# Band attention: turned edge blocks as float32, 128 columns wide, and one reciprocal per pair of query blocks

## The chip, the cores and the metric

The kernel runs on one core of a Trainium2 chip. The metric is the device time of one execution in microseconds (us). The engines are TensorE (PE, with its weight loads shown apart as PEld), VectorE (DVE), ScalarE (ACT), GpSimd (POOL) and SyncE (SP, which issues most transfers).

## What is computed

A trunk of two layers over 1024 tokens of width 1024. In each layer, a modulated RMSNorm, one input projection, three groups of attention heads (64 wide) side by side, an RMSNorm per group, one output projection with a gated residual, and a gated feed-forward part. The attention is what the change touches:

```python
# group A: 4 heads, 2-D neighbourhood (8 x 16) with a relative bias
# group B: 6 heads on 2 key heads, |i - j| <= 128, a sink logit, a shared relative bias
# group C: 6 heads on 2 key heads, dense
s = jnp.einsum('bnqgrd,bnkgd->bngrqk', qb, kb).astype(jnp.float32) * scale + bias
s = jnp.where(valid[None, :, None, None], s, NEG_INF)
p = jax.nn.softmax(jnp.concatenate([s, sink_logits], axis=-1), axis=-1)[..., :-1]
o = jnp.einsum('bngrqk,bnkgd->bnqgrd', p.astype(v.dtype), vb)
```

Groups A and B are the band groups: a block of 128 queries sees only its own block of 128 keys and the two next to it.

## The kernel before

**Precision.** Most products are made in float32r, a float32 format that the array multiplies at reduced precision. An operand that needs more is split into a rounded part and the rest (`split_pt`: ACT copies and rounds, DVE subtracts), and both parts are multiplied. Where an operand is declared plain float32, the array multiplies it as it is.

**The attention stage.** It walks through 64 pairs of query blocks per layer: 24 of group C (6 heads, 4 pairs each), then 16 of A and 24 of B. A pair p of a head is the query blocks 2p and 2p + 1, 256 columns in all. Each pair passes four steps: `qk` (scores on PE, the mask and bias or the row maximum on DVE, the exponential with its row sum on ACT, once for each of the two blocks c = 0, 1), the division (`divide`: a reciprocal on DVE, then `scale_rows` on POOL), `turn` (PE transposes the 128 x 128 blocks into PSUM, the copies bring them back) and `pv` (PE multiplies them by the values into the tile pv; `products` holds the loop, `combine` adds the two halves of the heads).

**The loop.** Iteration n turns pair n, multiplies pair n - 1 and scores pair n + 3 (group C) or n + 5 (band groups). Each iteration has two halves, i = 0, 1. What `finish` has put on the list `unfinished` is issued in the next half iteration, so the division of block c = 0 comes in the second half of an iteration and that of block c = 1 in the first half of the next. Only POOL's order is fixed as written in this stage (`pin((pool,), True)`); the instructions of the other engines are placed by a scheduler, and each engine then runs its own list in order.

**A band pair.** Of the four blocks of keys that a pair sees, the two inner ones are seen by both query blocks, the left outer one only by the first and the right outer one only by the second: these are the edges. Pairs p = 1, 2 have both edges, p = 0 only the right one, p = 3 only the left one. `turn(0)` turns the four inner blocks into one PSUM tile T and splits them into pt (two parts of 256 columns for each key block). `turn(1)` turns the one or two edges and splits them into the tile `edge`. Its two buffers are made once by `edges_make` (at n = 8) with the half that the edge does not fill set to zero, so that an edge is multiplied 256 columns wide like the inner blocks, rounded part and rest:

```python
movs = [(k0 + i, self.pt[0][:, i, :], self.pt[1][:, i, :]) for i in range(2)]
if self.left:
    movs.append((k0 - 1, e[:, 0, 0, :], e[:, 1, 0, :]))
if self.right:
    movs.append((k0 + 2, e[:, 0, 1, :], e[:, 1, 1, :]))
```

All engine calls pass through one helper, so that nearly all instructions of the profile carry line 49; the tiles tell them apart (sC, sA, sB: scores; pr: exponentials; rs: maxima, sums and reciprocals; T, pt, edge: turned blocks; pv, cmb, y: results).

Of the kernel before, what the change touches and what calls it, by code (L numbers as in the profile page):

```python
# [10 lines left out]
F32 = mybir.dt.float32  # L11
F32R = mybir.dt.float32r
# [7 lines left out]
P = 128  # L20
# [56 lines left out]
def f32(ap):  # L77
    return ap.bitcast(F32)
# [7 lines left out]
def trunk(ctx: ExitStack, tc, A, C, out):  # L86
    nc = tc.nc
    pe, act, dve, pool, sp = (
        Engine(tc, e) for e in (nc.tensor, nc.scalar, nc.vector, nc.gpsimd, nc.sync)
    )  # L90
# [28 lines left out]
    ident = idp.tile([P, P], F32, name="ident")  # L119
# [6 lines left out]
    ident, ones = f32(identr), f32(onesr[:, 0:1])  # L126
# [692 lines left out]
    for l in range(2):  # L819
# [212 lines left out]
        vs = vsp.tile([P, 8, 8, P], F32R, name="vs")  # L1032
# [95 lines left out]
        def scale_rows(pr, r):  # L1128
            pool.tensor_scalar(
                out=pr, in0=pr, scalar1=r, scalar2=1.0, op0=ALU.mult, op1=ALU.mult  # L1130
            )
# [14 lines left out]
                pr, s, AF.Exp, bias=rs[:, c : c + 1], accum_out=rs[:, 2 + c : 3 + c]  # L1146
            )

        def divide(pr, rs, c):
            dve.reciprocal(rs[:, 4 + c : 5 + c], rs[:, 2 + c : 3 + c])  # L1150
            scale_rows(pr, rs[:, 4 + c : 5 + c])

        first_pairs = []

        def early_scores():

            p = len(first_pairs)
# [11 lines left out]
            return lambda: [divide(prs[c], rs, c) for c in range(2)]  # L1169

        for oc in range(NE, 8):
            w = wab
            for half in range(2):
# [15 lines left out]
                i = 2 * (oc - NE) + half  # L1189
# [31 lines left out]
        zB = [bz_tile() for _ in range(2)]  # L1221
        pad(atp, 16)
        gss = {23: gss_tile()}
        edge = []

        def edges_make():
            for _ in range(2):
                e = atp.tile([P, 2, 2, 256], F32R, name="edge", tag="edge", bufs=2)
                for z in range(2):
                    pool.memset(f32(e[:, z, 0, 128:256]), 0.0)  # L1230
                    pool.memset(f32(e[:, z, 1, 0:128]), 0.0)
                edge.append(e)

        edges_used = [0]

        def next_edge():
            edges_used[0] += 1
            return edge[edges_used[0] % 2]

        def edge_ap(e, z, left, right):  # L1240
            flat = e[:, z, :, :].rearrange("p e q -> p (e q)")
            if left and right:
                return flat.rearrange("p (a q) -> p a q", a=4)[:, 0:4:3, :]
            return flat[:, None, 0:128] if left else flat[:, None, 384:512]

        def pt_tile():
            return wp.tile([P, 4, 256], F32R, name="pt", tag="whl", bufs=8)

# [3 lines left out]
        def rs_tile():  # L1252
            return atp.tile([P, 8], F32, name="rs", tag="rs", bufs=6)
# [4 lines left out]
        def split_pt(T, hi, lo):  # L1258
            act.copy(hi, T)
            dve.tensor_tensor(out=lo, in0=T, in1=f32(hi), op=ALU.subtract)  # L1260

        class Pair:
# [5 lines left out]
            def __init__(self, row, vh, p):  # L1268
                self.row, self.vh, self.p = row, vh, p
                self.rs = rs_tile()  # L1270

            def finish(self, c, pr):

                unfinished.append(lambda: divide(pr, self.rs, c))

            def products(self, movs, part):
                if part == 0:
                    if self.p % 2 == 0:
                        open_pv[0] = psV.tile([P, H], F32, name="pv", tag="V")
                    self.pvt = open_pv[0]  # L1280
                cols = slice((self.p % 2) * 256, (self.p % 2) * 256 + 256)
# [47 lines left out]
        class PairC(Pair):  # L1329
# [5 lines left out]
            def qk(self, c):  # L1335
                pr = self.pr[c] = pr_tile()
                c_scores(self.h, 2 * self.p + c, c, pr, self.rs)
                self.finish(c, pr)

            def turn(self, c):  # L1340
                if c == 0:
# [9 lines left out]
            def pv(self, part):  # L1351
                self.products(
                    [
                        (kb * 4 + i, self.pt[kb][0][:, i, :], self.pt[kb][1][:, i, :])
                        for kb in range(2)
                        for i in range(4)
                    ],
                    part,
                )
# [38 lines left out]
        class Band(Pair):  # L1398
# [10 lines left out]
            def qk(self, c):  # L1409
                rs, p, sk = self.rs, self.p, self.sk  # L1410
                if c == 0:
                    self.s = psS.tile([P, 2, 512], F32, name=self.name, tag="S")
                s, pr = self.s, self.pr
                j = 2 * p + c
                a, b = self.spans[c]
                for i in range(2):
                    pe.matmul(
                        s[:, c, a:b], self.q[:, j * P : (j + 1) * P],
                        self.k[i][:, (j - 1) * P + a : (j - 1) * P + b],
                        start=(i == 0), stop=(i == 1),  # L1420
                    )
# [12 lines left out]
                self.finish(c, pr[:, c, a:b])  # L1434

            def turn(self, c):
                pr = self.pr
                T = t_tile()
                if c == 0:
                    self.pt = [pt_tile() for _ in range(2)]  # L1440
                    for b in range(2):
                        for i in range(2):
                            pe.transpose(
                                T[:, 2 * b + i, :], pr[:, b, (1 - b + i) * P : (2 - b + i) * P],
                                ident,
                            )
# [6 lines left out]
                ne = 0  # L1453
                if self.left:
                    pe.transpose(T[:, ne, :], pr[:, 0, 0:P], ident)
                    ne += 1
                if self.right:
                    pe.transpose(T[:, ne, :], pr[:, 1, 2 * P : 3 * P], ident)
                    ne += 1
                split_pt(  # L1460
                    T[:, 0:ne, :],
                    edge_ap(e, 0, self.left, self.right),
                    edge_ap(e, 1, self.left, self.right),
                )

            def pv(self, part):
                k0, e = 2 * self.p, self.e
                movs = [(k0 + i, self.pt[0][:, i, :], self.pt[1][:, i, :]) for i in range(2)]
# [128 lines left out]
        for n in range(-AHEAD - 1, N + 1):  # L1597
# [22 lines left out]
                    (v_back if n else v_store)(j)  # L1620
            if n == 50:
                yq = qk_tile()
            if n == 8:
                edges_make()
            if n == 54:
                wst = [w_o_stage(k) for k in korder[:2]]
            if n in (55, 59):
# [735 lines left out]
```

## Time and profile before

| | us |
|---|---|
| median of 3 runs | 2432.55 (2431.05 to 2435.31) |
| the profiled execution | 2435.83 |
| its span, first to last instruction | 2434.1 |
| band groups of layer 0 in it, about | 375 to 487 |
| group C and band groups of layer 1, about | 1440 to 1570 and 1570 to 1685 |

The profile shows one execution. A group row reads: engine, operation, out<-in, sizes, xcount | busy us, mean ns of one | idle time of the engine just before them and what ended it. A wait row reads: who waited <- for whom: us in total, times, the longest. A chain row gives the share of the chain of work that ended last, by engine and tile. In rows of time, the start and the length of a run of like instructions stand first.

### The profile page before, as it was taken

The numbers are of one execution on the slowest core, as the hardware profiler recorded it, in microseconds if no ns is written. First come the engines' busy times: TensorE is split into PE (matmuls) and PEld (weight loads), VectorE is DVE, ScalarE is ACT, GpSimd is POOL, SyncE is SP. The second block draws the span as 40 slices with busy tenths as digits, with TensorE's granted clock in tenths as the row PEclk, the third lists the DMA queues.
The fourth block names the chain that finished last, engine by engine and source line by source line (L and its number), as shares of the span: only waits on it lengthen the run. The fifth ranks groups of instructions, "written<-read, shape, count | busy, mean of one in ns | idle before, by whom it ended". The sixth has DMA issues, their size and how long they took to land.

```text
span 2434.1 us, 33735 instructions
## 1 busy us (share of the span) xinstructions
PE 2362.9 (97%) x11733; PEld 1963.3 (81%) x11733; DVE 1785.1 (73%) x2950; ACT 1203.9 (49%) x2290; POOL 759.6 (31%) x741
## 2 busy tenths in 40 slices
PE   8999999999999999999999999999999999999998
PEld 5778888788788788788787879987877888888886
DVE  5756899976967788586677589998787545547865
ACT  3421788954543333344543148887454333334443
POOL 1530344620244444300036114464004444430001
PEclk9999999999999999999999999999999999999999
DMA  8478215154245454596434861242534422329643
GB/s 262 151 237 269 61 27 148 43 181 148 87 143 178 156 183 150 166 276 195 144 96 113 277 187 27 58 125 68 191 96 136 142 100 96 103 101 305 206 129 108
DMA packets 305338, 356.98 MB, mean 147 GB/s; under 512 B 51964, under 2 KB 221788, under 8 KB 305168
## 3 DMA queue, kind: packets, MB, share of 16 engines
q1 hardware_dynamic: 283296, 342.07, 44.5%
q10 hardware_dynamic: 21504, 12.59, 2.0%
q8 instruction: 93, 1.52, 0.3%
q14 instruction: 77, 0.63, 0.1%
q0 software_dynamic: 368, 0.17, 0.0%
HBM read 269.79 MB, written 88.63 MB: 147 GB/s over the span
## 4 chain that ended last, share of the span: by engine, by line
PE 50%; DVE 4%; issue 4%; ACT 2%; POOL 1%; DMA 1%; ACTq 0%; SPq 0%; POOLq 0%; DVEq 0%
PE ps_w L49 21%; PE ps_d L49 14%; PE ps_o L49 3%; PE pv L49 2%; PE ps_ab L49 2%; PE ps_v L49 2%; PE T L49 2%; PE sC L49 2%; DMA qkd<-qko 1%; ACT pr L49 1%; PE ps_c L49 1%; POOL ct L49 1%; DVE pt L49 0%; PE ps_st L49 0%; DVE pr L49 0%
## 5 line engine op out<-in xcount | busy, mean ns | idle before, releaser
L49 PE MATMUL ps_d<-wpt 128*128 128x512 f32 x1848 | 424.3, 390 | 2.2 <-ACT wpt L49 1.9
L49 PEld LDWEIGHTS ps_d<-wpt 128*128 128x128 f32 x1848 | 345.6, 188 | 76.2 <-issue 3.0
L49 POOL TENSOR_SCALAR pr<-pr,rs 128x1024 f32<-128x1024 f32 (+2 forms) x248 | 192.8, 780 | 228.8 <-DVE rs L49 203.2
L49 POOL TENSOR_TENSOR sg<-sg,u 128x512 f32<-128x512 f32 x86 | 125.8, 1465 | 356.5 <-ACT sg L49 117.9
L49 PE MATMUL pv<-pt,vs 128*128 128x256 f32 x1088 | 182.5, 296 | 10.8 <-DVE y L49 3.6
L49 ACT CAST wpt<-w 128x512 fp32r<-128x512 f32 x154 | 95.7, 621 | 179.9 <-PE ps_d L49 161.4
L49 DVE TENSOR_TENSOR pt<-T,pt 128x512 fp32r<-128x512 f32 x272 | 178.2, 681 | 6.9 <-ACT pt L49 5.1
L49 PE MATMUL T<-identr,pr 128*128 128x128 f32 x1176 | 172.8, 273 | 1.0 <-DVE pt L49 0.5
L49 ACT CAST pt<-T 128x512 fp32r<-128x512 f32 x272 | 153.0, 586 | 37.8 <-PE T L49 35.8
L49 ACT COPY u<-ps_w 128x512 f32<-128x512 f32 x128 | 75.1, 587 | 193.1 <-PE ps_w L49 192.9
L49 POOL TENSOR_TENSOR wpt<-ws,wpt 128x512 fp32r<-128x512 f32 x80 | 112.3, 1405 | 179.0 <-ACT wpt L49 132.5
L49 DVE TENSOR_TENSOR wpt<-w,wpt 128x512 fp32r<-128x512 f32 x154 | 108.9, 707 | 80.6 <-ACT wpt L49 78.4
L49 PEld LDWEIGHTS pv<-pt,vs 128*128 128x128 f32 x1088 | 145.3, 189 | 27.6 <-DVE y L49 9.8
L49 PEld LDWEIGHTS T<-identr,pr 128*128 128x128 f32 x1176 | 138.2, 140 | 18.3 <-POOL pr L49 1.3
L49 DVE SCALAR_TENSOR_TENSOR acc<-wmt,condT,acc 128x512 f32<-128x512 f32 (+1 forms) x98 | 116.9, 1201 | 44.2 <-DMA wmt<-in_w_mod_dram 43.7
L49 ACT CAST wpt<-ws 128x512 fp32r<-128x512 f32 x176 | 107.7, 622 | 63.4 <-issue 28.2
L49 DVE TENSOR_TENSOR wpt<-ws,wpt 128x512 fp32r<-128x512 f32 x96 | 82.3, 868 | 62.9 <-ACT wpt L49 62.8
L49 DVE TENSOR_TENSOR wpt<-graw,wpt 128x512 fp32r<-128x512 f32 x154 | 109.2, 709 | 19.3 <-ACT wpt L49 19.3
L49 ACT CAST wpt<-graw 128x512 fp32r<-128x512 f32 x154 | 95.0, 617 | 48.2 <-DMA graw<-gpd 40.3
L49 DVE TENSOR_TENSOR ws<-wr 128x512 f32<-128x512 f32 x88 | 80.0, 911 | 49.2 <-POOL wpt L49 46.0
L49 PE MATMUL ps_w<-h22h,wpt 128*128 128x512 f32 x352 | 111.6, 399 | 4.3 <-ACT sg L49 3.6
L49 DVE TENSOR_REDUCE rs<-sC 128x1 f32<-128x1024 f32 x88 | 107.1, 1218 | 7.1 <-PE sC L49 5.2
(299 smaller groups left out, 6024.5 us busy)
## 6 DMA issues: line engine op xcount, KB each, us to landing
wr<-in_w_gu_dram SPq DMA_DIRECT2D x92, 512.0 KB, 4.1
gpd<-sg SPq DMA_DIRECT2D x154, 256.0 KB, 4.4
graw<-gpd SPq DMA_DIRECT2D x76, 512.0 KB, 3.5
w<-in_w_down_dram SPq DMA_DIRECT2D x110, 256.0 KB, 5.4
wmt<-in_w_mod_dram SPq DMA_DIRECT2D x48, 512.0 KB, 6.1
qk<-qkd SPq DMA_DIRECT2D x44, 512.0 KB, 6.7
wst<-in_w_o_dram SPq DMA_DIRECT2D x32, 512.0 KB, 3.9
wmt<-in_w_mod_dram SPq DMA_DIRECT2D x64, 256.0 KB, 3.8
```

Source lines behind the costliest of these rows:

```text
L49: ins = op(*args, **kwargs)
```

## The change

The tile `edge` becomes plain float32, 128 columns for each edge, allocated for each pair from three buffers; the zero halves and `edges_make` go. A turned edge is copied once out of PSUM, by ACT for odd p and by DVE for even p, with no split. `products` takes for each key block the columns of the result and a list of moving operands: two parts of 256 columns for an inner block, one float32 operand of 128 columns for an edge, multiplied with the values read as plain float32. `divide` takes both blocks of a pair: `finish` gathers them and, after the second one, puts one division on the list, with one reciprocal over two columns and then the two scalings on POOL. This holds for all three groups.

```diff
-        def divide(pr, rs, c):
-            dve.reciprocal(rs[:, 4 + c : 5 + c], rs[:, 2 + c : 3 + c])
-            scale_rows(pr, rs[:, 4 + c : 5 + c])
+        def divide(prs, rs):
+            dve.reciprocal(rs[:, 4:6], rs[:, 2:4])
+            for c, pr in enumerate(prs):
+                scale_rows(pr, rs[:, 4 + c : 5 + c])
...
-            def finish(self, c, pr):
-
-                unfinished.append(lambda: divide(pr, self.rs, c))
+            def finish(self, pr):
+
+                self.parts.append(pr)
+                if len(self.parts) == 2:
+                    unfinished.append(lambda: divide(self.parts, self.rs))
...
-                for n, (kc, a, b) in enumerate(movs):
+                for n, (kc, at, mvs) in enumerate(movs):
                     if (n < half) != (part == 0):
                         continue
-                    for i, mv in enumerate((a, b)):
+                    for i, mv in enumerate(mvs):
+                        v = vs[:, kc, self.vh, :]
                         pe.matmul(
-                            self.pvt[:, cols], vs[:, kc, self.vh, :], mv,
-                            start=(n == 0 and i == 0), stop=(n == len(movs) - 1 and i == 1),
+                            self.pvt[:, c0 + at.start : c0 + at.stop],
+                            v if mv.dtype == F32R else f32(v), mv,
...
-                e = self.e = next_edge()
...
-                split_pt(
-                    T[:, 0:ne, :],
-                    edge_ap(e, 0, self.left, self.right),
-                    edge_ap(e, 1, self.left, self.right),
-                )
+                e = self.e = atp.tile([P, 2, P], F32, name="edge", tag="edge", bufs=3)
...
+                if self.p % 2:
+                    act.copy(e[:, 0:n], T[:, 0:n])
+                else:
+                    dve.tensor_copy(e[:, 0:n], T[:, 0:n])
...
-                    movs.append((k0 - 1, e[:, 0, 0, :], e[:, 1, 0, :]))
+                    movs.append((k0 - 1, slice(0, P), [e[:, 0]]))
...
-                    movs.append((k0 + 2, e[:, 0, 1, :], e[:, 1, 1, :]))
+                    movs.append((k0 + 2, slice(P, 2 * P), [e[:, int(self.left)]]))
```

More of the change, by code (lines that the diff above doesn't have):

```diff
@@ L1168, in early_scores @@
             first_pairs.append(prs)
-            return lambda: [divide(prs[c], rs, c) for c in range(2)]
+            return lambda: divide(prs, rs)
         for oc in range(NE, 8):
@@ L1223, in trunk @@
         gss = {23: gss_tile()}
[L1224 to L1244, printed above, removed]
         def pt_tile():
@@ L1270, in __init__ @@
                 self.rs = rs_tile()
-            def finish(self, c, pr):
-                unfinished.append(lambda: divide(pr, self.rs, c))
+                self.parts = []
+            def finish(self, pr):
+                self.parts.append(pr)
+                if len(self.parts) == 2:
+                    unfinished.append(lambda: divide(self.parts, self.rs))
             def products(self, movs, part):
@@ L1280, in products @@
                     self.pvt = open_pv[0]
-                cols = slice((self.p % 2) * 256, (self.p % 2) * 256 + 256)
+                c0 = (self.p % 2) * 256
                 half = (len(movs) + 1) // 2
-                for n, (kc, a, b) in enumerate(movs):
+                for n, (kc, at, mvs) in enumerate(movs):
                     if (n < half) != (part == 0):
                         continue
-                    for i, mv in enumerate((a, b)):
+                    for i, mv in enumerate(mvs):
+                        v = vs[:, kc, self.vh, :]
                         pe.matmul(
-                            self.pvt[:, cols], vs[:, kc, self.vh, :], mv,
-                            start=(n == 0 and i == 0), stop=(n == len(movs) - 1 and i == 1),
+                            self.pvt[:, c0 + at.start : c0 + at.stop],
+                            v if mv.dtype == F32R else f32(v), mv,
+                            start=(n == 0 and i == 0),
+                            stop=(n == len(movs) - 1 and i == len(mvs) - 1),
+                            skip_group_check=True,
                         )
@@ L1337, in qk @@
                 c_scores(self.h, 2 * self.p + c, c, pr, self.rs)
-                self.finish(c, pr)
+                self.finish(pr)
             def turn(self, c):
@@ L1353, in pv @@
                     [
-                        (kb * 4 + i, self.pt[kb][0][:, i, :], self.pt[kb][1][:, i, :])
+                        (kb * 4 + i, slice(0, 256), [t[:, i, :] for t in self.pt[kb]])
                         for kb in range(2)
@@ L1433, in qk @@
                 )
-                self.finish(c, pr[:, c, a:b])
+                self.finish(pr[:, c, a:b])
             def turn(self, c):
@@ L1451, in turn @@
                     return
-                e = self.e = next_edge()
[L1453 to L1459, printed above, removed]
-                split_pt(
-                    T[:, 0:ne, :],
-                    edge_ap(e, 0, self.left, self.right),
-                    edge_ap(e, 1, self.left, self.right),
-                )
+                e = self.e = atp.tile([P, 2, P], F32, name="edge", tag="edge", bufs=3)
+                n = 0
+                for left, here in ((True, self.left), (False, self.right)):
+                    if here:
+                        src = pr[:, 0, 0:P] if left else pr[:, 1, 2 * P : 3 * P]
+                        pe.transpose(T[:, n, :], src, ident)
+                        n += 1
+                if self.p % 2:
+                    act.copy(e[:, 0:n], T[:, 0:n])
+                else:
+                    dve.tensor_copy(e[:, 0:n], T[:, 0:n])
             def pv(self, part):
                 k0, e = 2 * self.p, self.e
-                movs = [(k0 + i, self.pt[0][:, i, :], self.pt[1][:, i, :]) for i in range(2)]
+                movs = [
+                    (k0 + i, slice(0, 2 * P), [t[:, i, :] for t in self.pt]) for i in range(2)
+                ]
                 if self.left:
-                    movs.append((k0 - 1, e[:, 0, 0, :], e[:, 1, 0, :]))
+                    movs.append((k0 - 1, slice(0, P), [e[:, 0]]))
                 if self.right:
-                    movs.append((k0 + 2, e[:, 0, 1, :], e[:, 1, 1, :]))
+                    movs.append((k0 + 2, slice(P, 2 * P), [e[:, int(self.left)]]))
                 self.products(movs, part)
@@ L1622, in trunk @@
                 yq = qk_tile()
-            if n == 8:
-                edges_make()
             if n == 54:
```

## The prediction

> **What bounds the kernel now.** I read the page first (busy shares, then the chain that ended last), then the stretches of time by engine, then the chain inside the stretches that the change touches.
>
> ```profile
> span 2434.1 us, 33735 instructions
> ...
> PE 2362.9 (97%) x11733; PEld 1963.3 (81%) x11733; DVE 1785.1 (73%) x2950; ACT 1203.9 (49%) x2290; POOL 759.6 (31%) x741
> ...
> PE 50%; DVE 4%; issue 4%; ACT 2%; POOL 1%; DMA 1%; ACTq 0%; SPq 0%; POOLq 0%; DVEq 0%
> ```
>
> Over the whole span TensorE leads. But these are averages over stages, and the change lives in the attention stage of each layer. The next view is the busy time by engine in three stretches: the band groups of layer 0, those of layer 1, and the dense group (C) of layer 1. Columns: stretch, its length, then PE, PEld, DVE, ACT, POOL.
>
> ```profile
> 375.00:487.00 112.00, 105.75 (x746) 92.75 (x745) 102.06 (x361) 101.36 (x277) 65.89 (x118) 1.00 0.38 103
> 1570.00:1682.00 112.00, 105.05 (x732) 91.23 (x731) 102.23 (x358) 101.51 (x277) 68.53 (x118) 1.00 0.34 94
> 1450.00:1570.00 120.00, 119.23 (x857) 108.30 (x856) 113.38 (x192) 102.95 (x191) 53.27 (x55) 1.00 0.14 36
> ```
>
> In the band groups VectorE is busy 91% and ScalarE 91% of the time, and PE has holes although its busy time counts pipelined matmuls long. In group C PE has no holes at all (119.2 of 120). The chain by line says who ends last: first the band groups of layer 1 (1570 to 1682), then their last third (1643 to 1665), then group C (1450 to 1570).
>
> ```profile
> by line: PE pv L49 14.7%; ACT pr L49 12.9%; PE T L49 7.5%; DVE pr L49 7.1%; issue 7.0%; PE sB L49 5.9%; PE sA L49 5.1%; DVE pt L49 4.8%; ACT pt L49 4.1%; POOL y L49 3.4%; POOL pr L49 3.3%; DVE y L49 3.0%; PE ps_st L49 3.0%; ACT cmb L49 2.9%
> ...
> by line: ACT pr L49 32.4%; ACT pt L49 12.7%; issue 12.1%; ACT cmb L49 9.4%; ACT edge L49 6.3%; POOL y L49 5.7%; ACT qk L49 5.7%; POOL pr L49 3.3%; ACT rb L49 2.8%; DVE pt L49 2.7%; PE pv L49 2.7%; ACT gss L49 2.5%; DVE pr L49 1.8%; DVE rs L
> ...
> by line: PE pv L49 33.9%; PE sC L49 29.6%; PE T L49 26.9%; DVE rs L49 2.2%; ACT pr L49 1.5%; DVE y L49 1.1%; issue 1.1%; DVE pt L49 1.0%; ACT pt L49 1.0%; ACT cmb L49 1.0%; PE sA L49 0.9%; DVEq L49 0.0%
> ```
>
> Group C is PE's. The band groups are nobody's: the chain changes hands, with stretches that are nearly all ScalarE. The first row names 84.7% of its chain: ACT 19.9 (pr, pt, cmb), DVE 14.9, PE 36.2. Scaled to the whole (divided by 0.847) and to 112 us, that is about 26.3 us on ACT, 19.7 us on DVE and 47.9 us on PE in one layer's band groups.
>
> **The edge copies.** There are 40 band pairs in a layer, 20 with one edge block and 20 with two. Now ACT rounds each turned edge out of PSUM and DVE subtracts to get the rest; after the change one of the two engines makes one plain copy, ACT for odd pairs (p = 1 with two blocks, p = 3 with one), DVE for even ones.
>
> ```profile
> L49 ACT CAST edge<-T 128x256 fp32r<-128x256 f32 x40 | 14.8, 369 | 1.9 <-PE T L49 1.4
> L49 ACT CAST edge<-T 128x128 fp32r<-128x128 f32 x40 | 10.5, 263 | 5.4 <-PE T L49 5.4
> L49 DVE TENSOR_TENSOR edge<-T,edge 128x256 fp32r<-128x256 f32 x40 | 16.5, 411 | 0.0
> L49 DVE TENSOR_TENSOR edge<-T,edge 128x128 fp32r<-128x128 f32 x40 | 11.2, 281 | 0.1
> ...
> L49 DVE COPY xt<-ps_x 128x512 f32<-128x512 f32 x4 | 2.5, 682 | 0.0
> L49 DVE TENSOR_TENSOR pt<-T,pt 128x512 fp32r<-128x512 f32 x272 | 178.2, 681 | 6.9 <-ACT pt L49 5.1
> ```
>
> ACT per layer: 20 x (0.369 + 0.263) = 12.6 us go, 10 x (0.369 + 0.263) = 6.3 us come (a plain copy in place of a rounding one, taken at the same price): 6.3 us less, 6.2% of its 101.5. DVE per layer: 20 x (0.411 + 0.281) = 13.8 us go. A DVE copy out of PSUM takes as long as the subtraction of the same size (682 and 681 ns at 512 columns), so 10 x (0.411 + 0.281) = 6.9 us come: 6.9 us less.
>
> **The reciprocals.** 64 pairs in a layer, each with two, now each with one over two columns.
>
> ```profile
> L49 DVE RECIPROCAL rs<-rs 128x1 f32<-128x1 f32 x248 | 38.8, 158 | 14.7 <-ACT pr L49 10.0
> ...
> L49 DVE RECIPROCAL gm<-gm 128x8 f32<-128x8 f32 x1 | 0.2, 203 | 0.4 <-ACT gm L49 0.4
> ```
>
> Two columns lie between one (158) and eight (203); by their slope it is 164 ns, so a pair saves 0.152 us: 6.1 us for the 40 band pairs and 3.6 us for the 24 of group C, all on DVE. With the edges DVE loses 13.0 us, 12.7% of its 102.2, in each layer's band groups.
>
> The merged reciprocal adds a wait: it stands in DVE's queue behind the exponential of the second block, and the mask additions, maxima and subtractions queued after it wait with it. The division factor of the first block comes later by one exponential and its read, 0.618 + 0.193 us, and POOL, whose order is fixed, then scales both blocks in one go, ahead of the sink columns of later pairs.
>
> ```profile
> L49 ACT ACTIVATE pr<-pr,rs 128x385 f32<-128x385 f32 x72 | 44.3, 618 | 0.7 <-POOL pr L49 0.6
> L49 ACT ACTIVATION_READ_ACCUMULATOR pr<-pr,rs 128x1 f32 x160 | 30.8, 193 | 0.0
> ...
> DVE rs L49 <- ACT pr L49: 4.3, 13, 0.5
> PEld T L49 <- POOL pr L49: 0.6, 3, 0.3
> ```
>
> The last two rows are waits in 1570 to 1682 (total, times, longest). A band pair is scored five pairs before it is turned, and a pair takes 112 / 40 = 2.8 us, so 14 us stand against 0.8 us of lateness: I book nothing. The DVE wait may halve with the number of reciprocals or double with their lateness: between -2 and +4 us a layer, taken as 0, because the merged instruction is issued half an iteration later than the first one was.
>
> **The edge products on PE.** 120 edge blocks in both layers. Now two float32r multiplications of 256 columns each (rounded part and rest, with a zero half); afterwards one float32 multiplication of 128 columns. What does float32 cost? The trace has three kinds of it: turns (T, one record for each call), row sums (ps_st, 48 calls in the code and 96 records) and the modulation rows (ps_mod from gm, 8 calls and 16 records). So a float32 product is two records, each with a weight load. Rows below are weight loads or matmuls in order of time: start, length of the run, count.
>
> ```profile
> L49 PE MATMUL ps_st<-onesr,gss 128*128 128x1 f32 x96 | 11.0, 245 | 0.0
> L49 PE MATMUL ps_mod<-gm,condT 128*1 128x512 f32 x16 | 8.2, 591 | 0.0
> ...
> 14.55 1.02 PE L49 MATMUL ps_mod<-gm,condT 128*1 128x512 f32 x2
> ...
> 403.35 1.93 PEld L49 LDWEIGHTS ps_st<-onesr,gss 128*128 128x128 f32 x16
> ...
> 343.34 0.68 PEld L49 LDWEIGHTS T<-identr,pr 128*128 128x128 f32 x6
> 343.99 1.01 PEld L49 LDWEIGHTS pv<-pt,vs 128*128 128x128 f32 x8
> ...
> 432.78 0.55 PEld L49 LDWEIGHTS pv<-edge,vs 128*128 128x128 f32 x4
> ```
>
> Streaming: 1.02 - 0.591 = 0.43 us for 512 columns of a float32 record, so 0.107 for 128. Loading: float32 loads follow each other every (1.93 - 0.19) / 15 = 0.116 us; turns, which stream 128 float32 columns behind each load, every (0.68 - 0.14) / 5 = 0.108; the float32r products every (1.01 - 0.19) / 7 = 0.117, the edge ones 0.12. Loads and streams overlap in all of them. A new edge record should take the longer of 0.116 and 0.107, as the old one does, and there are 240 of either: 0. The lower bound is the turns' pace, 240 x -0.009 = -2 us; the upper, if this kind does not overlap, 240 x 0.107 = +26 us. I take 0: ps_st has the same loads and T the same streams.
>
> The Trainium skill, page "TensorE: Matmul & The Clock Gate", section "The mechanism", says that a weight load overlaps running matmuls only where the row groups differ; these use all rows, so by it the record would cost load plus stream, and the sum the upper bound. The rows of T and pv speak against it here. The page "FP8 and Floating Point Precision" of the Trainium skill, section "TensorE Precision Notes", gives a true float32 product four passes; with a load of its own for each, 4 x 0.116 us stand against 2 x 0.117. The ps_st rows show two loads for a product, not four.
>
> **Small things.** 16 memsets go from POOL, which is busy 61% of the band groups and off the path; nothing is booked. Three edge buffers stand where there were two, and a turned edge's PSUM tile is free after one reader instead of two in a row. Waits for the edges were small (ACT for the turn, PE for the edges):
>
> ```profile
> ACT edge L49 <- PE T L49: 3.1, 9, 0.6
> PEld pv L49 <- ACT edge L49: 0.8, 1, 0.8
> PEld pv L49 <- DVE edge L49: 0.8, 2, 0.6
> ```
>
> That is 1.6 us of PE in a layer, inside the sum below.
>
> **The sum.** In the band groups the time that the chain spends on ACT and DVE shrinks with their load: 26.3 x 6.2% = 1.6 us, 19.7 x 12.7% = 2.5 us, together 4.1 us a layer. In group C DVE holds 4.3% of the chain (rs, y, pt), 5.2 us of 120, and loses 3.6 / 113.4 = 3.2%: 0.2 us. Two layers: 8.6 us, call it 8.8 with the halved edge waits. Nothing outside the attention stage changes. The profiled execution took 2435.83 us (span 2434.1 and 1.7 around it), 3.3 above the median 2432.55 of the three timed runs; I expect 2427.0 of a profiled execution and 2423.8 of the median. A difference of 0.2% (4.9 us) is about what a measurement of this kernel can tell from none.
>
> **Rivals.**
> *ACT sets the pace throughout.* The stretch 1643 to 1665 is that: three quarters of the chain are ACT and its issue gaps. If the whole of the band groups went with ACT's load, 2 x 6.3 = 12.6 us would go: 2420; with all of group C's DVE saving as well (7.2 us), 2413. Against it: PE holds 43% of the chain.
> *No change.* The instructions of group C and of the band groups are placed by a scheduler, and their order on every engine differs from the second C pair on (the built programs show it). The holes that ACT and DVE leave may be filled by waits for PE: 2428 to 2437, centre 2432.
> *Slower through PE.* Float32 loads and streams of the edges do not overlap: +12.9 us of PE a layer. PE's 732 records at 0.12 are 88 us of 112 and would become 101. By PE's share of the chain that costs 5.5 us, at most 12.9, less the 4.3 gained: +2 to +17 over both layers, taken as +10: 2442.6. It decides from 4.3 / 0.43 / 120 = 0.083 us more a record, a pace of 0.20. The turns and row sums speak against it.
> *Slower through the late division.* POOL's fixed order makes each pair's turn wait. At half of the longest such wait seen, 0.15 us for 128 pairs, 19 us come and 8.8 go: 2443. It decides from 0.07 us a pair. Against it: the lead of five pairs, in group C three.
>
> **How the numbers follow.** The forecast 0.44, ACT throughout 0.20, no change 0.20, PE 0.09, late division 0.07. Faster by over 0.2%: 0.64; within: 0.20; slower: 0.16. The range runs from most of the second case, 2414, over the forecast and the no-change case to 2436, and leaves out the two slower cases and the far ends.
>
> **What would show it.** In the changed profile: edge copies 20 + 20 on each of ACT and DVE at about 369 / 263 and 411 / 281 ns; 128 reciprocals near 164 ns; edge records of PE 240, their loads 0.116 to 0.12 us apart (0.2 or more means the PE rival); ACT's busy time in the band groups about 95 us, DVE's about 89, in a stage about 4 us shorter; group C unchanged within 1 us. PE turns waiting for POOL by more than some 5 us a layer would mean the late division. The forecast is wrong if ACT and DVE fall as said and the stage keeps its length.

## The result and the profile after

The changed kernel takes 2423.16 us (median of 10 runs, 2420.56 to 2430.54), the kernel before 2432.93 us (10 runs, 2429.54 to 2438.49) beside it: a ratio of 0.9965, 95% interval 0.9954 to 0.9975, or 9.8 us less. The forecast was 2423.8. The profiled execution took 2422.97 us. Its page, the lines that answer to those of before:

```profile
span 2421.1 us, 33439 instructions
...
PE 2350.5 (97%) x11733; PEld 1955.2 (81%) x11733; DVE 1766.8 (73%) x2782; ACT 1194.3 (49%) x2250; POOL 753.4 (31%) x725
...
PE 48%; DVE 4%; issue 4%; DMA 2%; ACT 2%; POOL 2%; ACTq 0%; SPq 0%; POOLq 0%; DVEq 0%
```

Over the span little shows. What can be measured well is the length of a stage between two marks. For the band groups I take the first score of group A (tile sA) and the start of the last copy of a head's half (tile cmb). The rows by tile give lowest / median / highest duration in ns, then the first and the last start. Layer 0, before and then after:

```profile
L49 PE MATMUL sA<-qk x64: 278/339/446, 374.7 to 420.5; 128*128 128x384 f32 x48, 128*128 128x256 f32 x16
L49 ACT COPY cmb<-pv x32: 577/581/587, 271.9 to 505.2; 64x512 f32<-64x512 f32 x32
```

```profile
L49 PE MATMUL sA<-qk x64: 278/338/446, 375.2 to 419.1; 128*128 128x384 f32 x48, 128*128 128x256 f32 x16
L49 ACT COPY cmb<-pv x32: 577/582/584, 272.8 to 498.6; 64x512 f32<-64x512 f32 x32
```

That is 505.2 - 374.7 = 130.5 us before and 498.6 - 375.2 = 123.4 after; in layer 1, by the same marks, 130.3 and 123.2. So the band groups are 7.1 us shorter in each layer, where 4.1 was forecast. Busy time in these very stretches (stretch, length, then PE, PEld, DVE, ACT, POOL), before and after:

```profile
374.70:505.20 130.50, 122.37 (x848) 106.57 (x847) 119.37 (x388) 113.69 (x301) 72.77 (x123) 1.00 0.36 102
```

```profile
375.20:498.60 123.40, 117.81 (x843) 103.86 (x842) 111.61 (x328) 108.91 (x281) 71.65 (x124) 1.00 0.38 108
```

DVE issues 60 instructions fewer (20 for the edges, 40 reciprocals), ACT 20 fewer. The shares hardly move (DVE 91 to 90%, ACT 87 to 88%, PE 94 to 95%): the same mixture runs faster, and no engine has taken over. The durations of the instructions that changed, grouped by shape, in the band groups of layer 0 after:

```profile
L49 PE MATMUL pv<-edge,vs 128*128 128x128 f32 x120 | 20.2, 274 | 0.0
L49 PEld LDWEIGHTS pv<-edge,vs 128*128 128x128 f32 x120 | 17.0, 190 | 0.0
L49 DVE RECIPROCAL rs<-rs 128x2 f32<-128x2 f32 x41 | 6.5, 160 | 1.4 <-ACT pr L49 1.1
L49 DVE COPY edge<-T 128x256 f32<-128x256 f32 x10 | 4.2, 415 | 0.0
L49 ACT COPY edge<-T 128x256 f32<-128x256 f32 x10 | 3.6, 364 | 0.4 <-PE T L49 0.4
L49 DVE COPY edge<-T 128x128 f32<-128x128 f32 x10 | 2.8, 277 | 0.0
L49 ACT COPY edge<-T 128x128 f32<-128x128 f32 x10 | 2.6, 262 | 0.6 <-PE T L49 0.6
```

These are the prices of the prediction (369/263 on ACT, 411/281 on DVE, 164 for the reciprocal). The weight loads of the edge products, in order of time, four in a row:

```profile
440.49 0.53 PEld L49 LDWEIGHTS pv<-edge,vs 128*128 128x128 f32 x4
```

That is (0.53 - 0.19) / 3 = 0.113 us from one to the next, no more than before (0.12). The chain in most of the band groups of layer 1 (1560 to 1672), and the waits there (1565 to 1670; who waited <- for whom: us, times, longest):

```profile
by line: PE pv L49 15.8%; ACT pr L49 14.2%; POOL pr L49 8.8%; issue 8.1%; PE T L49 8.0%; ACT pt L49 5.6%; PE sA L49 5.6%; ACT cmb L49 4.0%; DVE pr L49 3.9%; DVE pt L49 3.7%; DVE y L49 3.1%; PE sB L49 3.1%; PE ps_st L49 3.0%; POOL y L49 2.2%
```

```profile
POOL pr L49 <- DVE rs L49: 33.7, 21, 6.1
...
DVE rs L49 <- ACT pr L49: 1.1, 4, 0.3
...
PEld T L49 <- POOL pr L49: 0.4, 1, 0.4
```

DVE's share of the chain (pr, pt, y) falls from 14.9 to 10.7%, and POOL's scaling rises from 3.3 to 8.8%. But PE's turns wait for POOL no more than before (0.4 us, and 0.6 between 1565 and 1670 before), and DVE's wait for the exponential shrinks (1.1 us, 3.7 before).

Group C became longer, which was not forecast. I count it from the first product of a turned block (tile pv) to the first score of group A: before 257.8 to 374.7 in layer 0 and 1444.6 to 1561.5 in layer 1, 116.9 us in both; after 117.9 and 119.4.

### The profile page after: what moved, and what is told of

It is laid out like the page before. It is cut to its first block, busy times and chain, and to the rows that moved or that the text cites. A ratio compares the mean times of both kernels' runs of the same rounds, so it can differ in the third digit from the quotient of the medians.

```text
span 2421.1 us, 33439 instructions
## 1 busy us (share of the span) xinstructions
PE 2350.5 (97%) x11733; PEld 1955.2 (81%) x11733; DVE 1766.8 (73%) x2782; ACT 1194.3 (49%) x2250; POOL 753.4 (31%) x725
## 4 chain that ended last, share of the span: by engine, by line
PE 48%; DVE 4%; issue 4%; DMA 2%; ACT 2%; POOL 2%; ACTq 0%; SPq 0%; POOLq 0%; DVEq 0%
PE ps_w L49 21%; PE ps_d L49 14%; PE ps_o L49 3%; PE pv L49 2%; PE T L49 2%; PE ps_v L49 2%; PE sC L49 2%; DMA qkd<-qko 1%; ACT pr L49 1%; PE ps_c L49 1%; POOL ct L49 1%; PE ps_ab L49 0%; DVE acc L49 0%; DMA graw<-gpd 0%; POOL pr L49 0%
## 5 line engine op out<-in xcount | busy, mean ns | idle before, releaser
L49 POOL TENSOR_SCALAR pr<-pr,rs 128x1024 f32<-128x1024 f32 (+2 forms) x248 | 187.0, 768 | 227.8 <-DVE rs L49 212.8
L49 POOL TENSOR_TENSOR sg<-sg,u 128x512 f32<-128x512 f32 x86 | 125.5, 1461 | 354.5 <-ACT sg L49 117.9
L49 POOL TENSOR_TENSOR wpt<-ws,wpt 128x512 fp32r<-128x512 f32 x80 | 111.6, 1395 | 180.8 <-ACT wpt L49 133.9
L49 PEld LDWEIGHTS pv<-pt,vs 128*128 128x128 f32 x1088 | 143.9, 189 | 21.1 <-DVE y L49 11.1
L49 PEld LDWEIGHTS T<-identr,pr 128*128 128x128 f32 x1176 | 139.9, 140 | 19.7 <-ACT edge L49 2.2
```

What stands on the lines that cost most here:

```text
L49: ins = op(*args, **kwargs)
```

## The experiments

Three theories stood: that ACT and DVE share the pace with PE (the forecast), that ACT alone sets it, and that PE's edge records cost or save something. Later a fourth came, on group C. All lengths in us, layer 0 / layer 1. "By the stages" is the change of the band groups and of group C against the kernel before, both layers added up, from one profile; "timed" is the difference of the medians of runs on the same chip (the kernel before stood at 2433.67 beside e0 to e3, 2436.12 beside e4 to e7, 2433.11 beside e8 to e11).

| kernel | median | ratio to before, 95% | band groups | group C | by the stages | timed |
|---|---|---|---|---|---|---|
| before | 2432.93 | | 130.5 / 130.3 | 116.9 / 116.9 | | |
| changed | 2423.16 | 0.9965, 0.9954 to 0.9975 | 123.4 / 123.2 | 117.9 / 119.4 | -10.7 | -9.8 |
| e0 changed, again | 2422.60 | 0.9960, 0.9946 to 0.9974 | 123.7 / 123.4 | 119.5 / 117.9 | -10.1 | -11.1 |
| e1 edges only | 2430.20 | 0.9986, 0.9972 to 0.9999 | 126.9 / 126.8 | 119.9 / 117.7 | -3.3 | -3.5 |
| e2 reciprocal only | 2430.44 | 0.9981, 0.9969 to 0.9992 | 128.7 / 129.9 | 116.4 / 116.4 | -3.2 | -3.2 |
| e3 merged in bands only | 2424.79 | 0.9959, 0.9943 to 0.9974 | 123.3 / 123.6 | 118.4 / 120.0 | -9.3 | -8.9 |
| e4 edges all on ACT | 2424.45 | 0.9944, 0.9917 to 0.9971 | 124.4 / 124.4 | 117.8 / 119.4 | -8.6 | -11.7 |
| e5 edges all on DVE | 2424.30 | 0.9959, 0.9942 to 0.9975 | 126.1 / 125.8 | 117.9 / 117.9 | -6.9 | -11.8 |
| e6 float32, 256 wide | 2434.99 | 1.0002, 0.9987 to 1.0017 | 128.6 / 128.5 | 116.4 / 116.4 | -4.7 | -1.1 |
| e7 float32r, 128 wide | 2433.62 | 0.9994, 0.9984 to 1.0005 | 129.0 / 128.6 | 116.5 / 116.4 | -4.1 | -2.5 |
| e8 pool size kept | 2417.52 | 0.9943, 0.9927 to 0.9959 | 123.5 / 123.6 | 116.4 / 116.4 | -14.7 | -15.6 |
| e9 inner float32, even pairs | 2423.20 | 0.9960, 0.9945 to 0.9975 | 124.4 / 124.4 | 116.4 / 116.4 | -13.0 | -9.9 |
| e10 inner float32, all pairs | 2442.42 | 1.0033, 1.0020 to 1.0046 | 134.9 / 134.7 | 116.4 / 116.4 | +7.8 | +9.3 |
| e11 changed, third time | 2423.45 | 0.9965, 0.9951 to 0.9978 | 123.3 / 123.2 | 119.4 / 119.7 | -9.0 | -9.7 |

Stage lengths of the changed kernel agree within 0.5 us over three profiles, in the band groups, while whole runs scatter by several us. The two last columns agree within 1 us in seven rows and differ by 1.5 to 4.9 in the other six: the stretch from the last copy cmb of layer 0 to the first score of layer 1, which no edit touches, alone takes 913 to 927 us in the 14 profiles. So the stages carry the fine verdicts and the medians the coarse ones. The texts on record count group C from its first score, which takes in the end of the projections; that end (19 to 23 us) scatters by more than what is looked for, so the table leaves it out. This mark was chosen after e8, not before.

**e0: the changed kernel again**, no edit, as the reference beside e1 to e3.

> The changed kernel as it is, as the yardstick beside the others on one chip. It measured 2423.2 against 2432.9 (ratio 0.9965). Both theories expect 0.995 to 0.998 of the kernel before, the band groups from the first sA to the last combine about 123.3 us long in both layers (130.4 before) and group C of layer 0 from the first sC to the first sA about 140.4 (139.1 before).

The band groups repeat at 123.7 / 123.4. Group C is long again, but in the other layer.

**e1: the edges alone.** The division as before (its main line; `divide` too is that of before).

```diff
...
-                    unfinished.append(lambda: divide(self.parts, self.rs))
+                unfinished.append(lambda: divide(pr, self.rs, c))
```

> The float32 edges alone; every block keeps its own reciprocal and division. Theory 1 (the load taken from ACT and DVE sets the gain, edges and reciprocals alike): ACT loses 6.3 us a layer and DVE 6.9, by my shares of the chain 1.6 + 1.3 = 2.9 of 4.1 us a layer; scaled to the 7.1 that the trace shows, about 5.0 us a layer, 10 less in all for the band groups, 0 in group C (its order on PE is that of before up to the first band pairs): 2423. Theory 2 (the merged reciprocal costs in group C by its later division and brings its gain in the band groups): 7 us a layer minus what the reciprocals brought, group C back at 139.1; 2420 to 2424. Rival (the edges brought nothing and the new order of the merged division brought it all): 2432.

The band groups lose 3.5 us a layer: more than the 2.9 that the shares of the chain gave, less than the 5.0 scaled up from the whole change (and 2430.20 in all where 2423 was expected). Group C is longer although nothing in its work differs from before: whatever lengthens it is not the merged reciprocal.

**e2: the reciprocal alone.** The kernel before, with the merged `divide` and `finish`.

```diff
-            dve.reciprocal(rs[:, 4 + c : 5 + c], rs[:, 2 + c : 3 + c])
+            dve.reciprocal(rs[:, 4:6], rs[:, 2:4])
...
```

> The merged reciprocal alone, in all three groups; the edges stay in two float32r parts of 256 columns. Theory 1: DVE loses 6.1 us a layer in the band groups, worth 19.7 x 6% = 1.2, scaled by 7.1 / 4.1 about 2 us a layer; group C gains 0.2 a layer: 2428 to 2429. Theory 2: group C becomes 1.3 us longer in each layer and the band groups gain 1 to 2: 2431 to 2433, group C of layer 0 at 140.4. Rival: 2423, the whole of the gain.

1.8 and 0.4 us less in the band groups (forecast: 1.2 by the share, 2 scaled up), 0.5 less in group C (forecast: 0.2). With e1 that makes 4.6, but both together give 7.1: the merged reciprocal is worth 1.1 us beside the old edges and 3.5 beside the new ones. The two layers differ by 1.2 us in this profile, so the 1.1 is rough.

**e3: edges as changed, reciprocal merged in the band groups alone.**

```diff
...
+                self.parts.append(pr[:, c, a:b])
+                if c:
+                    unfinished.append(lambda: divide_pair(self.parts, rs))
```

> Float32 edges, the merged reciprocal in the band groups and one reciprocal for each block in group C. Theory 1 (group C's 1.3 us more is an accident of the order, worth nothing): the same as the changed kernel within 1.5 us, 2423. Theory 2 (the merged division costs in group C): group C of layer 0 back at 139.1 and the band groups at 123.3: 1.3 us a layer better than the changed kernel, about 2420.5.

The band groups have the whole gain (123.3 / 123.6), so all of it is made there; group C, with its old division, is long (118.4 / 120.0).

**e4 and e5: all edge copies on one engine.**

```diff
-                if self.p % 2:
-                    act.copy(e[:, 0:n], T[:, 0:n])
-                else:
-                    dve.tensor_copy(e[:, 0:n], T[:, 0:n])
+                act.copy(e[:, 0:n], T[:, 0:n])            # e4
+                dve.tensor_copy(e[:, 0:n], T[:, 0:n])     # e5
```

> The changed kernel with every edge copied by ACT. ACT's load is that of the kernel before (12.6 us of edge copies a layer), DVE loses 13.8 + 6.1. Theory 1 (both engines' loads count, each by its share of the chain): the band groups of the changed kernel, 123.4 us, become about 2.5 us longer by ACT and 2 us shorter by DVE: 123 to 125, all in all 2423 to 2426. Rival (ACT sets the pace): +6.3 us a layer, band groups 128 to 130, 2435. Rival (DVE sets it): 117 to 120 and 2415.

> The changed kernel with every edge copied by DVE. ACT loses 12.6 us a layer against the kernel before, DVE only 6.1. Theory 1: 123 to 125 in the band groups, 2423 to 2426. Rival (ACT sets the pace): 117 to 119, 2412. Rival (DVE sets it): 129 to 130, 2436.

Against the changed kernel the band groups are 1.1 us longer with all copies on ACT and 2.6 us longer with all on DVE. Theory 1 had 123 to 125 for both: e4 lies in it (124.4), e5 above it (126.1 / 125.8), but below the 129 of its rival. If either engine alone set the pace, clearing it wholly would have been the best of the three; the even split is. Against e2 (both engines loaded, the same reciprocals) e5 takes 12.6 us of rows off ACT for 3.3 us of stage, 0.27 a us; e4 takes 13.8 us off DVE for 4.9, 0.36 a us. These prices are no constants: by them the even split would gain 6.3 x 0.27 + 6.9 x 0.36 = 4.2 us on e2, and it gains 6.0.

**e6: float32 edges, kept 256 columns wide** with a zero half (the line for a left edge; the right one and three prepared buffers likewise).

```diff
...
-                    movs.append((k0 - 1, slice(0, P), [e[:, 0]]))
+                    movs.append((k0 - 1, slice(0, 2 * P), [e[:, 0]]))
```

> The changed kernel with float32 edges 256 columns wide (three prepared buffers with a zero half): the same copies and divisions, twice the streamed columns. A record then streams 256 float32 columns, 0.213 us by the modulation rows, in place of loading for 0.116: about 0.1 us more for 120 records a layer, 12 us of PE. Theory 1 (PE holds some 43% of the chain): the band groups become 5 us longer, 128 to 129, at most 12 (135); 2433. Rival (PE has slack and waits for the others anyway): 123 to 125, no change against the changed kernel. It also shows the pace of such records: 0.21 us.

The row of the edge products by tile, and four of their loads in a row:

```profile
L49 PE MATMUL pv<-edge,vs x240: 377/379/382, 393.7 to 1694.6; 128*128 128x256 f32 x120
...
443.51 0.74 PEld L49 LDWEIGHTS pv<-edge,vs 128*128 128x128 f32 x4
```

A record takes 379 ns, in the changed kernel 275 (median): 120 x 0.104 = 12.5 us of PE more a layer, and four loads take 0.74 us in place of 0.53. The band groups are 5.2 us longer than the changed kernel's: 0.42 us for each us of PE, where PE's share of the chain had said 0.43. This is the price of the rival "slower through PE", paid; the changed kernel doesn't pay it.

**e7: the edges as two float32r parts, 128 columns wide.**

```diff
...
+                split_pt(T[:, 0:n], e[:, 0, 0:n], e[:, 1, 0:n])
```

> The changed kernel with the edges split into two float32r parts as before (ACT rounds, DVE subtracts) but multiplied 128 columns wide, no zero half; merged reciprocal kept. The copies cost what they did before. Theory 1 (the copies are the gain and PE pays the weight load either way, 0.116 us a record): like the merged reciprocal alone, band groups 128.7 to 130, 2430. Rival (the width is the gain): 123 to 125, 2424. If a float32r record of 128 columns takes longer than 0.116 us, its pace shows it, and the band groups grow by PE's share of it.

```profile
L49 PE MATMUL pv<-edge,vs x240: 220/275/310, 392.0 to 1686.9; 128*128 128x128 f32 x120
...
448.94 0.53 PEld L49 LDWEIGHTS pv<-edge,vs 128*128 128x128 f32 x4
```

Half the width, and the record is as long as a float32 one of 128 columns (275), hardly shorter than 256 columns of float32r (282); the loads stand 0.113 us apart, as in the changed kernel. The band groups stand at 129, as in e2, which has the same copies: the width alone brings hardly anything (0.5 us on average), the gain is in the copies.

**e8: the changed kernel with the attention pool kept at its old size.** The smaller edge buffers (3 KB a partition in place of 8) move the tiles that are allocated after them by 5120 bytes. In e6 and e7 they move them by 2048. An unused tile puts the 5120 bytes back.

```diff
+            if n == 8:
+                atp.tile([P, 1280], F32, name="hold")
```

> The changed kernel with an unused tile of 1280 columns in the attention pool, so that the pool has the size of before and its tiles the addresses of before. In all kernels whose edge buffers take 3 KB (the changed one, edges alone, all on ACT, all on DVE) group C runs 279 to 282 us in the two layers together; in those with 6 or 8 KB 275 to 276. Their traces show DVE's first row maximum of layer 0's group C waiting 1.4 us for the stores of the query-key tile (qkd from qko): the tile rs lies on the last stored buffer there, on the one before in the others. Theory 1 (the addresses cause it): that wait goes, group C takes 275 to 277 in both layers, the band groups stay at 123.3: about 4 us less than the changed kernel, 2419. Rival (group C's length is scatter of the transfers): 279 to 282 again, 2423.

The trace had named a wait: the first row maximum of group C waits for a store of the projections' results (DVE in order of time; in brackets the idle time before and who ended it). After, then e8:

```profile
259.43 2.36 DVE L49 TENSOR_REDUCE rs<-sC 128x1 f32<-128x1024 f32 x2 [1.38 <-DMA qkd<-qko]
```

```profile
258.28 2.35 DVE L49 TENSOR_REDUCE rs<-sC 128x1 f32<-128x1024 f32 x2
```

By the addresses of the built programs, which no view of the profile shows, the tile rs falls on a buffer of qko, which holds results on their way out: in the kernel before on the last but one to be stored, in the changed kernel on the last one. The wait of 1.0 to 1.9 us stands in both layers of the changed kernel, e0, e1, e3, e4, e5 and e11, and in none of before, e2, e6, e7, e8, e9, e10. It delays the first exponentials, and so PE's next scores (PE's loads, after and e8):

```profile
261.95 0.76 PEld L49 LDWEIGHTS sC<-qk 128*128 128x128 f32 x4 [2.38 <-ACT pr L49]
```

```profile
260.79 0.77 PEld L49 LDWEIGHTS sC<-qk 128*128 128x128 f32 x4 [0.91 <-ACT pr L49]
```

In e8 the wait is gone and group C takes 116.4 us in both layers. The table shows the same split everywhere: 116.4 to 116.9 in the 14 layers without the wait, 117.7 to 120.0 in the 14 with it, on average 2.3 more. The timed medians say 5.9 us for both layers (e8 beside e11), the stages of the two profiles 5.7. The intervals of the ratios overlap, but five of the six runs of e8 (2415.82 to 2418.80) are below the fastest of the 24 runs of the changed kernel (2420.56). Two things in the e8 profile speak the other way. By the length from the first score, which the expectation used, it shows no gain: 139.7 and 139.8 us, the 279 to 282 of the rival. The part ahead of the first product takes 23.3 and 23.4 us there at a mean granted clock of 0.93, like layer 1 of e11 (23.3 us, 0.93); in the other 25 layers it takes 19.4 to 22.5 at 1.00. And the profiled execution of e8 is as long as that of e11 (2426.77 and 2426.50 us), because the stretch between the two attention stages took 920.7 us in it against 915.6; why isn't shown. The gain is thus well seen in group C and in the timed runs, its size less so. e8 is the fastest version of all: 15.6 us below the kernel before.

**e9 and e10: inner blocks as float32 too**, on top of e8, in even pairs or in all: one plain copy by ACT in place of the split, the products then float32, 256 wide.

```diff
+                    plain = self.p % 2 == 0     # e10: True
+                    if plain:
+                        t = self.pt[0] = f32(self.pt[0])
+                        act.copy(...)
+                        return
```

> The kernel with the kept pool size, and in even band pairs the inner blocks too are copied once as float32, by ACT, and multiplied as float32 (two records of 256 columns for each key block). Per layer 20 subtractions of 0.681 us leave DVE (13.6 us) and PE streams about 0.1 us more for 80 records (7.7 us). Theory 1 (each engine's load counts by its measured price: DVE about 0.36 us per us, PE 0.40): -4.9 + 3.1 = 1.8 us less a layer, band groups 121.5, 2415.5. Rival (with DVE and ACT relieved PE sets the pace): the band groups grow by up to 7 us, 125 to 130, 2423 to 2432.

> The same in all band pairs: 27 us less on DVE, 15.4 us more on PE a layer, DVE at some 62 of 105 us, PE's load and stream time at 103 of about 120. Theory 1 at the measured prices: -9.8 + 6.2 = 3.6 us less a layer, 120; but PE would then be busy 86% of it and its price rises: 120 to 128. Rival (PE sets the pace): 128 to 138 and 2428 to 2448.

Busy time in 105 us of the band groups of layer 0: e8, e9, e10.

```profile
375.00:480.00 105.00, 101.27 (x739) 90.50 (x740) 93.80 (x301) 95.36 (x257) 64.32 (x115) 1.00 0.41 110
```

```profile
375.00:480.00 105.00, 102.17 (x712) 91.80 (x711) 85.50 (x284) 94.45 (x255) 64.58 (x117) 1.00 0.37 100
```

```profile
375.00:480.00 105.00, 102.81 (x685) 91.33 (x683) 73.04 (x251) 88.12 (x234) 60.06 (x104) 1.00 0.40 110
```

DVE falls from 89% to 81 and 70%, and the stage does not get shorter: 0.9 us longer in e9, 11.3 in e10. e9 (124.4) lies between theory 1 (121.5) and its rival (125 to 130), e10 (134.9) in the range of the rival. e10's records of the inner blocks take 379 ns in place of 282, 160 of them in a layer: 15.5 us more on PE, so a us of PE now costs 0.73, after whatever the relief of DVE brings, and PE is busy 131.2 of the 134.9 us of the stage. The rival "PE sets the pace" is real, and begins just past the change.

**e11: the changed kernel a third time**, beside e8 to e10.

> The changed kernel beside the last three on the same chip, as their yardstick: 2422 to 2424, band groups 123.4, group C 279 to 282 in both layers together.

It repeats: 123.3 / 123.2, the wait in both layers, 2423.45.

## Why the prediction was right, and where it was not

**The time.** Forecast 8.8 us less, measured 9.8. It is right by two errors that cancel: the band groups gave 14.2 us where 8.2 were forecast, and group C took 3.5 where 0.4 were to come. The chance of faster came from the right mechanism, the load of ACT and DVE; the closeness is luck.

**The edge copies and reciprocals: right in price.** All instruction durations came out within 6 ns.

**The sum for the band groups: the step that was off is the adding up.** It took one gain for each engine, by its share of the chain and the load taken off, and added them: 1.6 us for ACT and 2.5 for DVE, 4.1 of the 7.1 measured. (The 112 us of the working are not the whole stage of 130.5; redone for the whole stage the sum stays at 4.2.) Singly the shares were fair: the edges alone, 2.9 by them, brought 3.5 (e1), the reciprocals alone, 1.2 by them, brought 1.8 and 0.4 (e2). But the two gains don't add: the same reciprocals bring 3.5 once ACT and DVE are rid of the edge splits. So a us of DVE has no one price: 19.7 / 102.2 = 0.19 by its share, 0.18 in e2, 0.36 in e4, 0.57 for the reciprocals beside the new edges. A us of ACT is worth 0.27 in e5 and 0.26 by its share. Nor is the share a fixed thing: ACT's exponentials hold 11.1% of the chain in layer 1's band groups before, 3.7 in e1, 9.3 in e2 and 12.9 after, by the same marks.

What makes the loads worth more together isn't shown. Three things go with the new edges and were not measured apart: every edge is spared one hop between ACT and DVE, its PSUM tile has one reader in place of two, and the scheduler orders each kernel anew. PE's listed waits for the edge copies hardly change (2.4 us in layer 0's stage before, 1.8 after), so neither of the first two shows as a wait of PE. e4 and e5 share both with the changed kernel, nothing but the load was edited in them, and their stages differ from its own: so the load does count.

The forecast of the busy time, DVE at about 89 us, was wrong in another way: it subtracted row durations. In the whole stage DVE's busy time fell by 7.8 us, not by 13.0, and ACT's by 4.8, not 6.3. Before, the 16 groups of DVE rows in that stretch add up to 143 us, with 119.4 busy, so rows overlap; after, they add up to 130.2, 12.8 less, as forecast, with 111.6 busy. A row taken out does not free all of its time. The wait of DVE for the exponential, taken as 0 between -2 and +4, fell by 3.3 us over the stage (4.4 to 1.1), but it falls as far in e1 (1.2) and e2 (1.3), so it does not explain why the two gain more together.

**PE's edge products: right.** The new records are as long as the old (275 and 282 ns), their loads follow each other as before (0.113 and 0.12 us), and the stage is not longer. The rival priced by no overlap needs 0.107 us more a record; e6 added that much and cost 5.2 us a layer. So the Trainium skill's rule (page "TensorE: Matmul & The Clock Gate", section "The mechanism") that a load overlaps only where the row groups differ does not hold for these records, which use all rows. The same section of the Trainium skill also lets a load that goes to a background weight buffer be pulled ahead; the prediction left that out, and no run here shows whether it is what happens.

**The late division: refuted.** PE's turns wait 0.4 us for POOL in a stage. POOL's scaling did come onto the chain, but not by the merging alone: by the same marks it holds 2.9% before, 5.1% in e1 without the merged reciprocal, at most 2.3% in e2 with it, and 8.0% after. The merged reciprocal gains in both comparisons, e2 beside the kernel before and the changed kernel beside e1.

**ACT throughout: refuted** by e4 and e5. Its stretch from 1643 to 1665 is even more ACT's than the prediction read: ACT and the issue gaps make 84% of that chain, not three quarters. **No change: refuted**: the holes were not filled by waits for PE, which is busy 94 and 95% of a stage that got shorter.

**Group C: "unchanged within 1 us" was wrong**, by 1.0 and 2.5 us. The step that failed is in "Small things": "three edge buffers stand where there were two" was read as a gain in freedom alone, but the buffers are smaller too, and with them what follows in the pool moved, by the addresses onto a buffer that was still being stored; e8 puts the size back, and the wait is gone. The merged reciprocal in group C itself gains 0.5 a layer (116.9 to 116.4 in e2 and e8).

## What to carry to other kernels

Where the pace is handed round between engines, relieve the others evenly, and try the work wholly on one and then wholly on the other: here the even split was better than both. An engine's share of the chain is a fair price for one small relief, but two reliefs that look independent can be worth more together, so run each alone and both. Stop when PE leads: one step further in the same direction (e9, e10) cost more than it brought. After any edit that changes a tile's size, look in the trace for new waits in stages that the edit didn't touch, since the tiles behind it have moved; putting the size back (e8) brought 5.9 us by the medians on top of the 9.8 of the change.

## What the runs showed of the hardware

**A pause of about 2 us can halve PE's clock for a while.** In the 14 layers with the wait PE pauses for 1.8 to 2.7 us before these scores, in the 14 without it for 0.7. Against a layer without the wait and with the same division in group C (116.9 us with two reciprocals, 116.4 with one), the wait costs 0.8 to 1.5 us in half of the layers that have it and 3.0 to 3.3 in the others. The changed kernel has one of each. Layer 0 and layer 1 of it, PE in order of time:

```profile
261.95 1.19 PE L49 MATMUL sC<-qk 128*128 128x512 f32 x4 [2.18 <-ACT pr L49]
...
1441.23 1.78 PE L49 MATMUL sC<-qk 128*128 128x512 f32 x4 [2.16 <-ACT pr L49]
```

The same pause, and the same four matmuls take 1.19 us or 1.78. Stretches of layer 1 of the same profile (the first of the last three columns is the granted clock):

```profile
1438.80:1441.20 2.40, 0.27 (x3) 0.06 (x1) 2.40 (x3) 1.23 (x3) 0.00 (x0) 1.00 0.06 19
1441.20:1442.20 1.00, 0.97 (x3) 0.83 (x4) 1.00 (x2) 1.00 (x2) 0.00 (x0) 0.70 0.00 0
1442.20:1443.20 1.00, 1.00 (x4) 0.70 (x4) 0.22 (x2) 0.56 (x2) 0.00 (x0) 0.50 0.00 0
1443.20:1444.20 1.00, 1.00 (x7) 1.00 (x6) 1.00 (x2) 0.30 (x1) 0.00 (x0) 0.50 0.00 0
1444.20:1445.20 1.00, 1.00 (x4) 0.77 (x4) 0.72 (x3) 1.00 (x2) 0.71 (x1) 0.59 0.33 82
1445.20:1447.20 2.00, 2.00 (x17) 1.86 (x16) 1.56 (x2) 1.27 (x4) 1.51 (x2) 1.00 0.58 221
```

At a clock of 1 outside it, a half clock that begins in the second row and ends in the fifth gives 0.6 + 1 + 1 + 0.82 = 3.4 us, about 1.7 us of work lost. Seven of the 14 layers with the wait show it (a mean clock of 0.72 in the six us from four us after the first product), and these are the seven with group C at 119.4 to 120.0 us; their pauses are 2.15 us and more. None of the 14 layers without the wait shows it in these six us, though the clock of 0.93 ahead of group C in e8 says that this wait is not the only occasion. The Trainium skill, page "TensorE: Matmul & The Clock Gate", section "What's actually happening", has the clock halve after an idle window of about 3.4 us and rise after a busy one of that length, in windows that run freely. The length of 3.4 us agrees, and so does the chance, but here 2.2 us of pause were enough, with PE at work before and behind it.

**Narrow float32r gains next to nothing.** A record of 128 columns takes 275 ns as float32r or float32; one of 256 takes 282 as float32r and 379 as float32 (medians of e7, the changed kernel, before, e6). Four loads in a row take 0.53 us at 128 columns in both formats, 0.55 at 256 of float32r and 0.74 at 256 of float32.
